# A decoder trunk whose feed-forward blocks use seven products: partial sums kept in PSUM, and products chained from block to block

## The chip, the cores and the metric

The kernel runs on one core of a Trainium2 chip. The metric is the device time of one execution in microseconds (us), lower being better. The core's engines are TensorE (PE, matmuls, with its weight loads shown as PEld), VectorE (DVE), ScalarE (ACT), GpSimd (POOL) and SyncE (SP, which issues most transfers). Matmul results are accumulated in PSUM, which has eight banks; a tile of 128 partitions by 512 float32 values fills one bank.

## What is computed

The reference is a two-layer decoder trunk on 512 tokens of width 1024. Each layer has a feed-forward stage, an attention mix (latent attention in the first layer, sparse attention in the second, both with memory heads), and a second feed-forward stage, each followed by a layer norm. The change touches the four feed-forward stages alone:

```python
def swiglu(x, w_gu, w_down):
    g, u = jnp.split(x @ w_gu, 2, axis=-1)
    return (jax.nn.silu(g) * u) @ w_down

x = layer_norm(DN_ALPHA * x + 0.5 * swiglu(x, w_gu, w_down), ln_g, ln_b)
```

The inner width is 2816, which is 22 chunks of 128 features. All values are float32. The kernel splits each operand into a high part and the remainder (`split`: ACT casts the high part, DVE subtracts to get the low part) and sums three matmuls, high by high, high by low and low by high.

## The kernel before

**Feed-forward.** `ffn` walks over five groups of chunks (`GROUPS`): a letter `s` is a chunk computed directly (`single`), a letter `d` one computed by seven products (`seven`). There are 77 chunks of the second kind in 20 groups of two to five. After a group's chunks come its down products (`by_units`, in the last group `token_major`), which add into the residual through DVE.

A seven-product chunk wants a gate (`gs`) and an up half (`us`) of 128 features for 512 tokens. Each is a sum over two halves of the input features, and the tokens are split in two halves of 256. So there is a 2x2 by 2x2 block product, which a Strassen-Winograd scheme does with seven quarter products in place of eight. Each quarter product (`quarter`, lines 398, 399 and 402) is 12 matmuls of 256 columns into one half of a bank. The token side of the products (`F.t[1]` to `F.t[5]`, and quarters of `xhi`, `xlo`) is formed once per stage. The weight side is formed for each chunk in `combined` (lines 147 to 153) from two loaded tiles, as four units: `g0` (as loaded), `g1` (a sum), `g2` (the difference of that and `g0`) and `g3` (half a unit).

Numbered as in the scheme, the products of a chunk are P1 (`g0`, lower half), P2 (`g0`, upper half), P3 (`g3`), P4 and P5 (`g1`), P6 and P7 (`g2`). Before the change each goes to a half bank of its own: P1 and P2 share a bank, P4 and P5 another, P6 and P7 a third, P3 has a fourth. The sums are made outside PE. ACT copies P1 to `us` (line 581) and DVE makes seven quarter-width adds with one operand in PSUM (lines 582, 591 to 595 and 599). Then ACT does one Silu over 512 columns (line 556), DVE the product with `us` (line 557) and the split into `hhi` and `hlo`.

**Order.** Weights are prepared in the order of `_unit_order`: SP loads a raw tile (`wraw`, four buffers), DVE combines where needed, ACT and DVE split it into `whi` and `wlo`, which have seven buffers in turn (`ring`: three and four). `unit` hands the next one to the products and asks for preparation four units ahead. The program's order is a priority only: a planner lays out each engine's queue from it by when it estimates that operands and buffers are ready, and sets all semaphores. An engine then works its queue in that order. The eight banks are taken round robin (`fbank`), four per chunk.

The lines of the profile speak of helpers: line 201 is every cast of `split`, line 202 every subtraction, lines 434 to 439 are the down products, lines 383 to 388 the directly computed chunks.

Of the kernel before, what the change touches and what calls it, by code (L numbers as in the profile page):

```python
# [9 lines left out]
F32 = mybir.dt.float32  # L10
# [3 lines left out]
ALU = mybir.AluOpType  # L14
# [41 lines left out]
def _unit_order():  # L56
# [2 lines left out]

    def ffn(l, f, s):  # L60
        for m0, items in _groups(l, f):
            m = m0
            for it in items:
                if it == "d":
                    order.extend((f"g{i}", (l, f, m), 1024, s) for i in range(4))
                else:
                    order.extend(("gu", (l, f, m, g), 1024, s) for g in range(2))
                m += 1
            for i in range(m0, m):
                order.append(("dn", (l, f, i), 1024, s))  # L70

# [36 lines left out]
def tile_trunk(ctx: ExitStack, tc, a: dict, out):  # L108
# [12 lines left out]
    class W:  # L121
# [4 lines left out]
        count = 0  # L126
        early = 0
        ready = {}

    def load(src, n=1024):  # L130
        raw = wraw.tile([P, 1024], F32, name="wraw")
# [3 lines left out]
    def combined(name, idx):  # L135


        l, f, m = idx
        lo, up = slice(0, 512), slice(512, 1024)
        op = nc.vector.tensor_tensor  # L140
        if name == "g0":
            W.g = load(a["gu"][l, f, m, 0])
            return W.g
        if name == "g1":
            W.u = load(a["gu"][l, f, m, 1])
            W.s = wraw.tile([P, 1024], F32, name="wraw")
            op(W.s[:, up], W.g[:, lo], W.u[:, lo], op=ALU.subtract)
            op(W.u[:, lo], W.u[:, lo], W.u[:, up], op=ALU.add)
            return W.u
        if name == "g2":  # L150
            op(W.s[:, lo], W.u[:, lo], W.g[:, lo], op=ALU.subtract)
            return W.s
        op(W.g[:, up], W.g[:, up], W.s[:, lo], op=ALU.subtract)
        return W.g[:, up]

    def ring(scope):
        pool, tag = wring, "r"
# [79 lines left out]
    def psum_pool(side, name):  # L237

        old = getattr(PS, side + "_st", None)
        if old is not None:  # L240
            old.close()
        st = ExitStack()
        pool = st.enter_context(tc.tile_pool(name=f"{name}_{side}", bufs=1, space=PSUM, side=side,
                                             reuse_waits="tile"))
        setattr(PS, side, pool)
        setattr(PS, side + "_st", st)

    def bank(i):
        i %= 8
# [82 lines left out]
    def norm_tile(t, st, spill=None, final=False):  # L332
# [15 lines left out]
        def turn():  # L348
            for h in range(2):
                pt = bank((2 * t if t < 2 else 6) + h)  # L350
                for c in range(4):
# [39 lines left out]
    def quarter(ps, w, off, xh, xl, first=None):  # L391


        hi, lo = w
        fh, fl = first or (xh, xl)
        for k in range(4):
            ks = slice(off + k * P, off + (k + 1) * P)
            nc.tensor.matmul(ps, lhsT=hi[:, ks], rhs=(xh if k else fh)[:, k], start=k == 0, stop=False)  # L398
            nc.tensor.matmul(ps, lhsT=hi[:, ks], rhs=(xl if k else fl)[:, k], start=False, stop=False)  # L399
        for k in range(4):  # L400
            ks = slice(off + k * P, off + (k + 1) * P)
            nc.tensor.matmul(ps, lhsT=lo[:, ks], rhs=xh[:, k], start=False, stop=k == 3)  # L402

    def quarters(k, c):
        v = (slice(None), slice(4 * k, 4 * k + 4), slice(256 * c, 256 * c + 256))
# [2 lines left out]
    def token_forms():  # L408
# [52 lines left out]

    def by_units(names, lhs, on_tile, b, look):


        n = len(names)
        tiles = [(b // 2 + i) % NT for i in range(NT)]
# [63 lines left out]
    def ffn(l, f, i, halves, spill=None, final=False, mid=None, hook=None):  # L530
# [14 lines left out]
        for gi, (m0, items) in enumerate(groups):  # L545
# [22 lines left out]
            def seven(j, t4):  # L568

                c0, c1 = slice(0, 256), slice(256, 512)  # L570
                gs = hp.tile([P, T], F32, tag="sg", name="gs", bufs=3)
                us = hp.tile([P, T], F32, tag="sg", name="us", bufs=3)
                op = nc.vector.tensor_tensor
                w0 = unit("g0", (l, f, m0 + j), 4)
                w = unit("g1", (l, f, m0 + j), 4) if t4 == 4 else None
                p12, p45 = fbank(), fbank()
                if t4 == 4:
                    quarter(p45[:, c0], w, 512, *F.t[5 if gi else 4], F.t[4])
                quarter(p12[:, c0], w0, 0, *quarters(0, 0))
                quarter(p12[:, c1], w0, 512, *quarters(1, 0))  # L580
                nc.scalar.copy(us[:, c0], p12[:, c0])
                op(gs[:, c0], us[:, c0], p12[:, c1], op=ALU.add)
                if t4 == 5:
                    w = unit("g1", (l, f, m0 + j), 4)
                    quarter(p45[:, c0], w, 512, *F.t[5])
                quarter(p45[:, c1], w, 0, *F.t[1])
                w = unit("g2", (l, f, m0 + j), 4)
                p67 = fbank()
                quarter(p67[:, c0], w, 0, *F.t[2])
                quarter(p67[:, c1], w, 512, *F.t[3])  # L590
                op(us[:, c0], us[:, c0], p67[:, c0], op=ALU.add)
# [4 lines left out]
                w = unit("g3", (l, f, m0 + j), 4)  # L596
                p3 = fbank()
                quarter(p3[:, c0], w, 0, *quarters(1, 1))
                op(gs[:, c1], gs[:, c1], p3[:, c0], op=ALU.add)
                evac(j, gs, us, gs)  # L600

            j, opened = 0, False
            if gi == 0:
                forms = token_forms() if halves else F.forms
            if gi == 0 and halves:
                ws, ps = [], []
                for j in range(3):
                    for g in range(2):
                        ws.append(unit("gu", (l, f, m0 + j, g), 0))
                        ps.append(fbank())  # L610
                if hook is not None:
                    hook()
# [14 lines left out]
            for it in items:  # L627
                if gi == 0:
                    next(forms, None)
                if it == "d":  # L630
                    if gi == 0:
                        for _ in forms:
                            pass
                        if 5 not in F.t:
                            second_t4()
                    seven(j, 5 if opened else 4)
                    opened = True
                else:
                    single(j)
                j += 1  # L640

            last = gi == len(groups) - 1
            if gi == 2 and mid is not None:
# [971 lines left out]
```

## Time and profile before

| | |
|---|---|
| runs shown | 1841.46, 1841.88 and 1844.01 us, median 1841.88 |
| profiled execution, first to last instruction | 1840.9 us |
| mean granted clock of TensorE | 0.997 |
| busy: PE, PEld, DVE, ACT, POOL | 1822.2, 1641.0, 1462.0, 867.6, 168.5 us |
| matmuls | 12748, of which 6468 belong to the seven-product chunks |
| read from HBM | 188.16 MB, 106 GB/s over the span |

The profiled execution is known by its span alone; the runs' times also hold what lies around the span, which is 1.0 us by the median. A row that groups instructions gives the line, engine, operation, tiles written and read, shapes and count, then the busy time in us, the mean of one in ns, and after the last bar the idle time of that engine just before them with what ended it. A row of the timeline gives start and length in us. "Idle before" is time without an instruction on the engine, and the matmuls' ends are modelled.

### The profile page before, as it was taken

To read this page: it belongs to the slowest core of one execution; us is meant where nothing else is said; L and a number is where in the kernel's file an instruction comes from. 1 tells how busy PE (TensorE), PEld (TensorE's weight loads), DVE (VectorE), ACT (ScalarE), POOL (GpSimd) and SP (SyncE) were. 2 spreads that over 40 slices of the span, in tenths; PEclk is the share of its full clock that TensorE was granted. 3 is DMA by queue.
4 is the path that set the end of the run, shared out by engine and by line. 5 is a ranking of instruction groups with operands and counts; after the bars stand their busy time and mean duration, and the time that the engine had idled before them with its cause. 6 is when DMAs were issued, how large, how long until landed. Compare 5 with 4: busy or idle time off the path is not lost.

```text
span 1840.9 us, 31942 instructions
## 1 busy us (share of the span) xinstructions
PE 1822.2 (99%) x12748; PEld 1641.0 (89%) x12748; DVE 1462.0 (79%) x2364; ACT 867.6 (47%) x1440; POOL 168.5 (9%) x216
## 2 busy tenths in 40 slices
PE   9999999999999999999999999999999999999998
PEld 8899899996789899999998998998956699999997
DVE  8798788758668789788887987987667487887987
ACT  6344345456545335334753433444566354434432
POOL 0000000025500000000100000001266200000000
PEclk9999999999999999999999999999999999999999
DMA  7333335531135233234443323334321324323322
GB/s 267 115 115 110 120 104 152 185 104 33 61 114 173 80 103 127 81 104 149 130 154 104 127 84 112 115 122 160 109 50 25 114 87 145 115 81 115 122 80 74
DMA packets 61669, 208.05 MB, mean 113 GB/s; under 512 B 7152, under 2 KB 8320, under 8 KB 61520
## 3 DMA queue, kind: packets, MB, share of 16 engines
q1 hardware_dynamic: 57568, 194.46, 32.3%
q0 software_dynamic: 3520, 11.16, 1.8%
q8 instruction: 100, 1.64, 0.4%
q14 instruction: 49, 0.40, 0.1%
q10 hardware_dynamic: 432, 0.39, 0.1%
HBM read 188.16 MB, written 7.34 MB: 106 GB/s over the span
## 4 chain that ended last, share of the span: by engine, by line
PE 93%; DVE 2%; ACT 2%; DMA 1%; issue 1%; POOL 1%; POOLq 0%; SPq 0%; DVEq 0%; ACTq 0%
PE bank L398 13%; PE bank L399 13%; PE bank L402 13%; PE bank L435 5%; PE bank L434 5%; PE bank L436 5%; PE bank L437 5%; PE bank L438 5%; PE bank L439 5%; PE bank L383 3%; PE bank L388 3%; PE bank L385 3%; PE tb L715 3%; PE o L743 2%; PE bank L371 2%; PE bank L370 2%
## 5 line engine op out<-in xcount | busy, mean ns | idle before, releaser
L201 ACT CAST whi<-wraw 128x1024 fp32r<-128x1024 f32 (+2 forms) x475 | 460.6, 978 | 534.5 <-PE bank L439 239.5
L202 DVE TENSOR_TENSOR wlo<-wraw,whi 128x1024 fp32r<-128x1024 f32 (+2 forms) x475 | 535.0, 1129 | 125.8 <-ACT whi L201 124.8
L399 PE MATMUL bank<-t,whi 128*128 128x256 f32 x956 | 229.3, 276 | 0.0
L398 PE MATMUL bank<-t,whi 128*128 128x256 f32 x956 | 229.2, 276 | 0.0
L398 PE MATMUL bank<-xhi,whi 128*128 128x256 f32 x924 | 220.9, 276 | 0.0
L399 PE MATMUL bank<-xlo,whi 128*128 128x256 f32 x924 | 220.9, 276 | 0.0
L399 PEld LDWEIGHTS bank<-t,whi 128*128 128x128 f32 x956 | 179.5, 188 | 0.6
L398 PEld LDWEIGHTS bank<-t,whi 128*128 128x128 f32 x956 | 179.5, 188 | 0.6
L399 PEld LDWEIGHTS bank<-xlo,whi 128*128 128x128 f32 x924 | 173.5, 188 | 0.0
L398 PEld LDWEIGHTS bank<-xhi,whi 128*128 128x128 f32 x924 | 173.5, 188 | 0.0
L328 DVE SCALAR_TENSOR_TENSOR x<-x,bank 128x512 f32<-128x512 f32 x176 | 112.1, 681 | 53.3 <-PE bank L438 51.6
L402 PE MATMUL bank<-t,wlo 128*128 128x256 f32 x940 | 144.9, 276 | 0.0
L402 PE MATMUL bank<-xhi,wlo 128*128 128x256 f32 x924 | 142.3, 276 | 0.0
L434 PE MATMUL bank<-whi,hhi 128*128 128x512 f32 x336 | 131.1, 391 | 0.0
L435 PE MATMUL bank<-whi,hhi 128*128 128x512 f32 x336 | 131.0, 390 | 0.0
L436 PE MATMUL bank<-wlo,hhi 128*128 128x512 f32 x336 | 130.9, 389 | 0.0
L438 PE MATMUL bank<-whi,hlo 128*128 128x512 f32 x336 | 130.8, 389 | 0.0
L439 PE MATMUL bank<-whi,hlo 128*128 128x512 f32 x336 | 130.8, 389 | 0.0
L437 PE MATMUL bank<-wlo,hhi 128*128 128x512 f32 x336 | 130.7, 389 | 0.0
L383 PE MATMUL bank<-xhi,whi 128*128 128x256 f32 x520 | 124.8, 281 | 0.2 <-ACT whi L201 0.2
L402 PEld LDWEIGHTS bank<-t,wlo 128*128 128x128 f32 x940 | 124.1, 188 | 0.0
L385 PE MATMUL bank<-xlo,whi 128*128 128x256 f32 x520 | 123.6, 279 | 0.3 <-DVE xlo L202 0.3
(347 smaller groups left out, 3864.4 us busy)
## 6 DMA issues: line engine op xcount, KB each, us to landing
wraw<-in_gu SPq DMA_DIRECT2D x173, 512.0 KB, 3.4
wraw<-in_dn SPq DMA_DIRECT2D x88, 512.0 KB, 3.8
wraw<-in_wo SPq DMA_DIRECT2D x16, 512.0 KB, 4.4
wraw<-in_wm SPq DMA_DIRECT2D x8, 512.0 KB, 4.0
x_dram<-x SPq DMA_DIRECT2D x8, 512.0 KB, 2.6
x<-x_dram SPq DMA_DIRECT2D x8, 512.0 KB, 4.4
wraw<-in_w SPq DMA_DIRECT2D x8, 512.0 KB, 3.8
wraw<-in_wq SPq DMA_DIRECT2D x6, 512.0 KB, 4.3
```

What stands on the lines that cost most here:

```text
L201: nc.scalar.copy(hi, src)
L202: return eng.tensor_tensor(lo, src, hi.bitcast(F32), op=ALU.subtract).ins
L383: nc.tensor.matmul(ps[:, c0:c1], lhsT=hi[:, k * P:(k + 1) * P], rhs=F.xhi[:, k, c0:c1], start=k == 0, stop=False)
L398: nc.tensor.matmul(ps, lhsT=hi[:, ks], rhs=(xh if k else fh)[:, k], start=k == 0, stop=False)
L399: nc.tensor.matmul(ps, lhsT=hi[:, ks], rhs=(xl if k else fl)[:, k], start=False, stop=False)
L402: nc.tensor.matmul(ps, lhsT=lo[:, ks], rhs=xh[:, k], start=False, stop=k == 3)
L434: nc.tensor.matmul(p0, lhsT=ahi, rhs=hi[:, 0:512], start=first, stop=False)
L435: nc.tensor.matmul(p1, lhsT=ahi, rhs=hi[:, 512:1024], start=first, stop=False)
L436: nc.tensor.matmul(p0, lhsT=ahi, rhs=lo[:, 0:512], start=False, stop=False)
L437: nc.tensor.matmul(p1, lhsT=ahi, rhs=lo[:, 512:1024], start=False, stop=False)
L438: nc.tensor.matmul(p0, lhsT=alo, rhs=hi[:, 0:512], start=False, stop=last)
L439: nc.tensor.matmul(p1, lhsT=alo, rhs=hi[:, 512:1024], start=False, stop=last)
```

## The change

The seven sums move into PSUM. A product may now accumulate into the bank of an earlier one (`start=False`), and where a partial sum is needed twice, ACT copies it from its bank to the next one (`seeded`) and PE goes on accumulating on the copy. Each partial sum has a bank of its own, in which the upper half is used (`own`). With P1 in r1, r2 is a copy of r1; r1 takes P2 and is then the first half of the gate. r2 takes P6. In a group's later chunks r3 is a copy of r2 at this point and takes P4, while r2 takes P5, is read by DVE, and takes P3, which gives the gate's second half. P7 is copied to `us` by ACT, and DVE adds r2 and r3 to it. In a group's first chunk P4 has a bank to itself instead, and r2 is copied to `sg` in SBUF and added by DVE. Silu reads the banks directly, in two halves.

A matmul without `start` adds only where an earlier matmul has written the bank since it was last cleared; `PS.set` keeps account of the banks for which that holds, and `seeded` puts in one matmul where it doesn't.

The products of neighbouring chunks are interleaved: the first product (P1) of the following chunk is issued in the middle of the current one, its second (P2) just before the current P3. The order of the products is P4 P1 P7 P2 P6 P1' P5 P2' P3 in a group's first chunk, P6 P7 P1' P5 P4 P2' P3 in a middle one and P6 P7 P5 P4 P3 in the last (a prime marks the following chunk). The order of the weight units follows: `g0 g1 g2 g0' g3`, then `g2 g0' g1 g3`. `combined` keeps the raw tiles of two chunks apart (`W.pairs`), and the token form of P4 changes its sign, so that P4 is added.

```diff
@@ ffn of _unit_order
-                if it == "d":
-                    order.extend((f"g{i}", (l, f, m), 1024, s) for i in range(4))
...
+            for i in range(m, end):
+                names = ("g0", "g1", "g2", "+", "g3") if i == m else ("g2", "+", "g1", "g3")
+                for name in names:
+                    if name != "+":
+                        order.append((name, (l, f, i), 1024, s))
+                    elif i + 1 < end:
+                        order.append(("g0", (l, f, i + 1), 1024, s))
@@ token_forms
-        u = less(u, b[1, 0])
+        u = less(b[1, 0], u)
         form(4, u)
@@ ffn
-                quarter(p12[:, c0], w0, 0, *quarters(0, 0))
-                quarter(p12[:, c1], w0, 512, *quarters(1, 0))
-                nc.scalar.copy(us[:, c0], p12[:, c0])
-                op(gs[:, c0], us[:, c0], p12[:, c1], op=ALU.add)
...
-                op(us[:, c0], us[:, c0], p67[:, c0], op=ALU.add)
-                op(gs[:, c1], us[:, c0], p45[:, c1], op=ALU.add)
-                op(us[:, c0], us[:, c0], p67[:, c1], op=ALU.add)
-                op(us[:, c1], us[:, c0], p45[:, c1], op=ALU.add)
-                op(us[:, c0], us[:, c0], p45[:, c0], op=ALU.subtract)
...
-                op(gs[:, c1], gs[:, c1], p3[:, c0], op=ALU.add)
-                evac(j, gs, us, gs)
+                def own():
+                    PS.set.add(F.bk % 8)
+                    return fbank()[:, c1]
+
+                def seeded(src, w):
+                    bits = F.bk % 8 in PS.set
+                    r = own()
+                    if not bits:
+                        nc.tensor.matmul(r, lhsT=w[0][:, 0:P], rhs=F.xhi[:, 0, c0], start=True, stop=True)
+                    nc.scalar.copy(r, src)
+                    return r
+
+                def m1(j):
+                    if j not in w0:
+                        w0[j] = unit("g0", (l, f, m0 + j), 4)
+                    r1[j] = own()
+                    quarter(r1[j], w0[j], 0, *quarters(0, 0))
+                    r2[j] = seeded(r1[j], w0[j])
+
+                def m2(j):
+                    quarter(r1[j], w0[j], 512, *quarters(1, 0), start=False)
+                    sg[j] = hp.tile([P, T], F32, tag="sg", name="sg", bufs=3)
+                    nc.scalar.activation(sg[j][:, c0], r1[j], AF.Silu)
+
+                def p7(j, w):
+                    e = own()
+                    quarter(e, w, 512, *F.t[3])
+                    nc.scalar.copy(us[j][:, c0], e)
+
+                def p5(j, w):
+                    quarter(r2[j], w, 0, *F.t[1], start=False)
+                    op(us[j][:, c1], us[j][:, c0], r2[j], op=ALU.add)
+
+                def p3(j):
+                    w = unit("g3", (l, f, m0 + j), 4)
+                    quarter(r2[j], w, 0, *quarters(1, 1), start=False)
+                    nc.scalar.activation(sg[j][:, c1], r2[j], AF.Silu)
...
+                    if n == 0:
...
+                        r3 = own()
+                        quarter(r3, w, 512, *F.t[5 if gi else 4], F.t[4])
+                        m1(j)
+                        ws = unit("g2", (l, f, m0 + j), 4)
+                        p7(j, ws)
+                        m2(j)
+                        quarter(r2[j], ws, 0, *F.t[2], start=False)
+                        nc.scalar.copy(sg[j][:, c1], r2[j])
+                        if following is not None:
+                            m1(following)
+                        p5(j, w)
+                        op(us[j][:, c0], us[j][:, c0], r3, op=ALU.add)
+                        op(us[j][:, c0], us[j][:, c0], sg[j][:, c1], op=ALU.add)
+                    else:
+                        ws = unit("g2", (l, f, m0 + j), 4)
+                        quarter(r2[j], ws, 0, *F.t[2], start=False)
+                        r3 = seeded(r2[j], ws)
+                        p7(j, ws)
+                        if following is not None:
+                            m1(following)
+                        w = unit("g1", (l, f, m0 + j), 4)
+                        p5(j, w)
+                        quarter(r3, w, 512, *F.t[5], start=False)
+                        op(us[j][:, c0], us[j][:, c0], r3, op=ALU.add)
+                    if following is not None:
+                        m2(following)
+                    p3(j)
+                    finish(j)
```

More of the change, by code (lines that the diff above doesn't have):

```diff
@@ L61, in ffn @@
         for m0, items in _groups(l, f):
-            m = m0
-            for it in items:
-                if it == "d":
-                    order.extend((f"g{i}", (l, f, m), 1024, s) for i in range(4))
-                else:
-                    order.extend(("gu", (l, f, m, g), 1024, s) for g in range(2))
-                m += 1
+            m = m0 + items.count("s")
+            for i in range(m0, m):
+                order.extend(("gu", (l, f, i, g), 1024, s) for g in range(2))
+            end = m0 + len(items)
+            for i in range(m, end):
[5 more added lines that the diff above has]
+                        order.append(("g0", (l, f, i + 1), 1024, s))
+            m = end
             for i in range(m0, m):
@@ L141, in combined @@
         if name == "g0":
-            W.g = load(a["gu"][l, f, m, 0])
-            return W.g
-        if name == "g1":
[L145 to L149, printed above, removed]
-        if name == "g2":
[L151 to L154, printed above, removed]
+            W.pairs[idx] = [load(a["gu"][l, f, m, 0])]
+            return W.pairs[idx][0]
+        raws = W.pairs[idx]
+        if len(raws) == 1:
+            g, u, d = raws[0], load(a["gu"][l, f, m, 1]), wraw.tile([P, 1024], F32, name="wraw")
+            raws += [u, d]
+            op(d[:, up], g[:, lo], u[:, lo], op=ALU.subtract)
+            op(u[:, lo], u[:, lo], u[:, up], op=ALU.add)
+        g, u, d = raws
+        if name == "g1":
+            return u
+        if name == "g2":
+            op(d[:, lo], u[:, lo], g[:, lo], op=ALU.subtract)
+            return d
+        del W.pairs[idx]
+        op(g[:, up], g[:, up], d[:, lo], op=ALU.subtract)
+        return g[:, up]
     def ring(scope):
@@ L246, in psum_pool @@
         setattr(PS, side + "_st", st)
+        PS.set = set()
     def bank(i):
@@ L350, in turn @@
                 pt = bank((2 * t if t < 2 else 6) + h)
+                PS.set.discard((2 * t if t < 2 else 6) + h)
                 for c in range(4):
@@ L389, in feature_major, with quarter @@
                              start=False, stop=k == NKT - 1)
-    def quarter(ps, w, off, xh, xl, first=None):
+    def quarter(ps, w, off, xh, xl, first=None, start=True):
         hi, lo = w
@@ L462, in by_units @@
     def by_units(names, lhs, on_tile, b, look):
+        PS.set.update(range(8))
         n = len(names)
@@ L566, in single, with sevens @@
                 evac(j, *pp)
[L568 removed]
+            def sevens(js):
                 c0, c1 = slice(0, 256), slice(256, 512)
[L571 to L572 removed]
                 op = nc.vector.tensor_tensor
[L574 to L578, printed above, removed]
[L579 to L600 removed]
@@ L602, in ffn @@
-            j, opened = 0, False
+                us, sg, w0, r1, r2 = {}, {}, {}, {}, {}
+                def own():
+                    PS.set.add(F.bk % 8)
+                    return fbank()[:, c1]
[6 more added lines that the diff above has]
+                    return r
@@ new lines, in finish @@
+                def finish(j):
+                    g = sg[j]
+                    nc.vector.scalar_tensor_tensor(g, g, 0.5, us[j], op0=ALU.mult, op1=ALU.mult)
+                    split(hhi[:, j, :], hlo[:, j, :], g)
+                for n, j in enumerate(js):
+                    us[j] = hp.tile([P, T], F32, tag="sg", name="us", bufs=3)
+                    following = js[n + 1] if n + 1 < len(js) else None
+                    if n == 0:
+                        w0[j] = unit("g0", (l, f, m0 + j), 4)
+                        w = unit("g1", (l, f, m0 + j), 4)
[19 more added lines that the diff above has]
+                            m1(following)
+                        w = unit("g1", (l, f, m0 + j), 4)
+                        p5(j, w)
[5 more added lines that the diff above has]
+                    finish(j)
@@ L603, in ffn @@
+            j = 0
             if gi == 0:
@@ L609, in ffn @@
                         ws.append(unit("gu", (l, f, m0 + j, g), 0))
+                        PS.set.add(F.bk % 8)
                         ps.append(fbank())
@@ L630, in ffn @@
                 if it == "d":
[L631 to L639, printed above, removed]
-                j += 1
+                    break
+                single(j)
+                j += 1
+            if gi == 0:
+                for _ in forms:
+                    pass
+                second_t4()
+            sevens(range(j, n))
             last = gi == len(groups) - 1
```

9 lines of the change are left out of this document (6 added, 3 removed).

## The prediction

> **What bounds the kernel now.** I read the page's totals and chain first, then TensorE's product lines, then stretches of the feed-forward stages.
>
> ```profile
> PE 1822.2 (99%) x12748; PEld 1641.0 (89%) x12748; DVE 1462.0 (79%) x2364; ACT 867.6 (47%) x1440; POOL 168.5 (9%) x216
> PE 93%; DVE 2%; ACT 2%; DMA 1%; issue 1%; POOL 1%; POOLq 0%; SPq 0%; DVEq 0%; ACTq 0%
> ```
>
> TensorE (PE) works 1822.2 of 1840.9 us and makes 93% of the chain. A busy PE may still be badly fed, so next come the groups of the product helper (lines 398, 399, 402); the last column is PE's idle time before them.
>
> ```profile
> L399 PE MATMUL bank<-t,whi 128*128 128x256 f32 x956 | 229.3, 276 | 0.0
> L398 PE MATMUL bank<-t,whi 128*128 128x256 f32 x956 | 229.2, 276 | 0.0
> L398 PE MATMUL bank<-xhi,whi 128*128 128x256 f32 x924 | 220.9, 276 | 0.0
> L399 PE MATMUL bank<-xlo,whi 128*128 128x256 f32 x924 | 220.9, 276 | 0.0
> L402 PE MATMUL bank<-t,wlo 128*128 128x256 f32 x940 | 144.9, 276 | 0.0
> L402 PE MATMUL bank<-xhi,wlo 128*128 128x256 f32 x924 | 142.3, 276 | 0.0
> L398 PE MATMUL bank<-t5h,whi 128*128 128x256 f32 x276 | 66.5, 277 | 0.0
> L399 PE MATMUL bank<-t5l,whi 128*128 128x256 f32 x276 | 66.3, 276 | 0.0
> L402 PE MATMUL bank<-t5h,wlo 128*128 128x256 f32 x292 | 45.0, 276 | 0.0
> ```
>
> The counts add up to 6468, which is 77 seven-product blocks of 84 matmuls. Not one of them is preceded by measurable idle time. So there is no wait in these blocks that could be removed.
>
> ```profile
> 153.00:162.52 9.52, 9.52 (x87) 9.52 (x86) 9.36 (x16) 5.32 (x8) 0.00 (x0) 1.00 0.43 132
> 152.00:170.00 18.00, 18.00 (x161) 18.00 (x161) 17.81 (x30) 9.75 (x13) 0.00 (x0) 1.00 0.35 117
> 361.00:366.00 5.00, 5.00 (x45) 5.00 (x44) 2.25 (x2) 2.18 (x5) 0.00 (x0) 1.00 0.87 351
> 125.50:134.50 9.00, 9.00 (x42) 7.43 (x41) 8.09 (x14) 2.57 (x4) 0.00 (x0) 1.00 0.19 61
> 137.00:146.00 9.00, 9.00 (x41) 7.47 (x40) 3.37 (x5) 2.73 (x3) 0.00 (x0) 1.00 0.18 58
> ```
>
> The columns are length, then busy time (and count) of PE, weight load, VectorE (DVE), ScalarE (ACT) and GpSimd, then PE's granted clock. Inside the blocks PE passes a 256-column matmul about every 0.113 us (18.00 us, 161 counted with about two cut at the edges), so a product of 12 takes 1.36 us and a block of seven 9.52 us. DVE is full there: 9.36 of 9.52 us. It is full and yet holds nobody up.
>
> **The change part by part.** *Matmuls.* Each block still runs seven products of 12: 0 us. A seed put into a bank without its bits costs one extra matmul, 0.113 us. The down products of the inner groups mark all eight banks as set and every product adds its own, so I count one such place, after the shared K/V stage, where the transposes have taken banks out of the set: 0.1 us.
>
> *DVE and ACT work.* Durations are min/median/max in ns, then mean ns in the last two rows.
>
> ```profile
> L581 ACT COPY us<-bank x77: 354/363/371, 45.9 to 1804.7; 128x256 f32<-128x256 f32 x77
> L591 DVE TENSOR_TENSOR us<-us,bank x77: 407/415/422, 50.9 to 1809.6; 128x256 f32<-128x256 f32 x77
> L556 ACT ACTIVATE gs<-gs 128x512 f32<-128x512 f32 x77 | 48.8, 634 | 79.7 <-DVE gs L599 79.7
> L201 ACT CAST whi<-wraw 128x1024 fp32r<-128x1024 f32 x387 | 404.4, 1053 | 370.1 <-PE bank L439 163.7 <-PE bank L399 108.4 <-DVE wraw L148 49.7
> ```
>
> A block has seven quarter adds now; afterwards it has three (first of a group, 20 groups) or two (the other 57). That is 20x4 + 57x5 = 365 adds less, at 0.415 us 151 us of DVE time, all of it under the gapless PE: worth 0 us. DVE falls to about 9.36 - 5x0.415 = 7.3 us per block. ACT gains two copies (0.73 us) and has its one 512-wide Silu cut in two halves (not in the trace; each between the 0.36 of the copy and the 0.63 of the whole; I take the copy's): 5.3 becomes about 6.1 us per block. This too lies under PE; uncovered it would cost 0.8 us x 77 = 62 us, but only PE's own waits can bring that out.
>
> *New waits of PE.* This is the price. Before, nothing that ACT or DVE did with a bank was needed by PE again until the bank came round. Afterwards PE writes a bank again after ACT or DVE has read it, and accumulates on ACT's copy. Counting products that lie between the read's cause and PE's next write:
> - first block of a group: one product in each of four places (second product after the seed copy; fifth after the copy to `sg`; the following block's second after its seed; third after DVE's add);
> - last block: one product in two places (fifth after the seed of r3; third after DVE's add);
> - the 37 middle blocks: two or more everywhere.
>
> So 120 waits have a cover of 1.36 us, of which 80 on ACT and 40 on DVE. What does a reply take? Two fences, DVE then ACT, each with PE's start of the next product (the second PE row of the first):
>
> ```profile
> 114.05 0.62 PE L402 MATMUL bank<-t,wlo 128*128 128x256 f32 x4
> 114.50 0.28 PE L398 MATMUL bank<-xhi,whi 128*128 128x256 f32 x1
> 114.70 0.42 DVE L591 TENSOR_TENSOR us<-us,bank 128x256 f32<-128x256 f32 x1 [0.25 <-PE bank L402]
> ...
> 124.02 0.28 PE L398 MATMUL bank<-xhi,whi 128*128 128x256 f32 x1
> 125.38 0.41 DVE L591 TENSOR_TENSOR us<-us,bank 128x256 f32<-128x256 f32 x1
> ...
> 174.38 0.28 PE L398 MATMUL bank<-xhi,whi 128*128 128x256 f32 x1
> 175.13 0.41 DVE L591 TENSOR_TENSOR us<-us,bank 128x256 f32<-128x256 f32 x1
> ```
>
> ```profile
> 151.26 0.28 PE L398 MATMUL bank<-t,whi 128*128 128x256 f32 x1
> 151.58 0.36 ACT L581 COPY us<-bank 128x256 f32<-128x256 f32 x1
> ...
> 118.58 0.28 PE L398 MATMUL bank<-t5h,whi 128*128 128x256 f32 x1
> 119.33 0.36 ACT L581 COPY us<-bank 128x256 f32<-128x256 f32 x1
> ...
> 17.50 1.05 ACT L201 CAST whi<-wraw 128x1024 fp32r<-128x1024 f32 x1 [2.64 <-DMA wraw<-in_gu]
> 18.61 0.38 PE L383 MATMUL bank<-xhi,whi 128*128 128x256 f32 x1 [0.22 <-ACT whi L201]
> ```
>
> A free DVE starts 0.20 us into the next product (114.70 - 114.50), a free ACT 0.32 us in. PE follows a release by about 0.05 us (18.61 after 17.50 + 1.05). So DVE may be late by 1.36 - 0.20 - 0.42 - 0.05 = 0.69 us and ACT by 1.36 - 0.32 - 0.36 - 0.05 = 0.63 us before PE stops. Seen lateness: DVE 0, 1.16 and 0.55 us in the three places, which is 0, 0.47 and 0 us of stall, mean 0.16; ACT 0.43 us in the second place, behind a weight cast: no stall. Behind a whole cast just begun ACT would be 1.05 us late: 0.42 us of stall.
>
> Where they fall: the first block follows the down products, where DVE is busy 3.37 of 9.00 us and ACT 2.73, so I take 0 for its 80 waits. For the last block I take the mean of the three rows, 20 x 0.16 = 3.1 us, and halve it because DVE then has two idle us per block where it had 0.16: 1.6 us. For its seed I let one in ten meet a fresh cast: 20 x 0.42 / 10 = 0.8 us. The middle blocks allow 1.36 us more, which none of these rows reaches: 0. Bounds: below 0; above, all 20 last blocks paying both (20 x 0.89 = 17.8 us) and all 20 first ones the DVE stall (9.4 us): 27 us. I take 1.6 + 0.8 because the ordinary rows lie within the allowance.
>
> What is queued behind a late copy: on ACT the weight casts, needed by PE a block later; on DVE the low halves of those weights. Neither is urgent, unless rival B holds.
>
> The Trainium skill ("ScalarE: Activation LUTs", the step-by-step section) says that ACT writes to PSUM with less latency than to SBUF. No row here has ACT writing PSUM; by it the seed copies are shorter than 0.36 us, ACT's allowance grows and its 0.8 us shrinks towards 0.
>
> *Elsewhere.* The planner may order the attention stages a little differently. PE's listed waits, nearly all of them there, sum to about 10 us, the longest being
>
> ```profile
> PE tb L715 <- POOL pp L1317: 2.2, 1, 2.2
> ```
>
> I take 0 and allow 2 us either way.
>
> **Sum.** 0.1 + 0 + 1.6 + 0.8 = 2.5 us on a span of 1840.9. The median of the runs, 1841.88, lies 1.0 us above the span, which is launch and end around it and stays. So 1841.9 + 2.5 = 1844.4 us, +0.14%. A measurement of this kernel can tell about 0.2%, 3.7 us, so I forecast no change that can be measured.
>
> **Rivals.**
>
> *A, slower: the one-product covers don't hold.* It decides from 0.69 us of lateness on DVE and 0.63 on ACT, in the last block of each group. For it: 1.16 us is already seen on DVE, and ACT works more than before. Against: DVE has become freer. If half of the 20 last blocks pay 0.89 us and some first ones too, it is 9 us: 1851; if all do, 18 us: 1860. Chance 0.30.
>
> *B, slower: weights late.* The new order holds three raw buffers of a block and the next block's first one at once, which is all four.
>
> ```profile
> wraw<-in_gu SPq DMA_DIRECT2D x173, 512.0 KB, 3.4
> L151 DVE TENSOR_TENSOR wraw<-wraw 128x512 f32<-128x512 f32 x77 | 52.7, 684 | 0.5
> L202 DVE TENSOR_TENSOR wlo<-wraw,whi 128x1024 fp32r<-128x1024 f32 (+2 forms) x475 | 535.0, 1129 | 125.8 <-ACT whi L201 124.8
> ACT whi L201 <- PE bank L399: 185.9, 177, 2.6
> ```
>
> If the next load must wait for the last of them, a block's preparation is load 3.4, three combinations 2.05, cast 1.05 and three low halves 3.4 us, with 2.2 us of other DVE work between: 12.1 against PE's 9.52, 2.6 us lost per following block. The seven ring buffers let a unit's cast start eight products (10.9 us) ahead of its use, which after cast and low half (2.2) leaves 8.7 us. That absorbs the 3 x 2.6 of a group of four and not the 4 x 2.6 of the four groups of five: 4 x 1.7 = 7 us, and some more where a seed queues on ACT behind a cast that waits for DVE. Against: the difference's buffer comes back before the two low halves, and today casts wait for PE, not for data (the last row). 1850, chance 0.09.
>
> *C: it doesn't do what it says.* If seeds needed a matmul in every place (77 + 57 seeds), 134 x 0.113 = 15 us: 1857. Against: the set of banks above. Chance 0.03.
>
> *D, faster.* If DVE's reads of PSUM slowed the matmuls, fewer of them would speed PE up. The stretches above speak against it: 42 matmuls in 9.00 us with DVE at 8.09 and 41 with DVE at 3.37; 161 in 18.00 and 45 in 5.00 us at a full and a half-empty DVE. What is left is 2 us or more of PE's waits elsewhere and noise: 1837, chance 0.08.
>
> The Trainium skill ("TensorE: Matmul & The Clock Gate", Back-to-back issue gap) gives 256 columns 256/2.4 + 2.5 = 109.2 ns where the trace has 113; by that rule 6468 x 4 ns = 26 us would be open, and the time 1816, if the change touched what takes them. The stretches say that it does not.
>
> **How the numbers follow.** No change 0.50, at 1844.4 (own range 1839 to 1846); A 0.30, B 0.09, C 0.03, D 0.08. Faster is D, 0.08; slower A, B and C, 0.42. The range reaches down to the 2 us of the other stages, 1839.5, and up through A's half case to most of its full one, 1857; about 0.05 is left out below and 0.1 above.
>
> **What would show it.** Right: the idle time before the product lines stays under 3 us in all, DVE loses about 150 us of busy time, and the blocks keep 9.52 us. A: PE waits that name ACT's copy or DVE's add in the last blocks. B: PE waiting for weights, or ACT's casts waiting for the weight differences in most blocks. C: more than a few matmuls beyond 12748. Wrong altogether: matmuls in the blocks at a pitch other than 0.113 us.

## The result and the profile after

The changed kernel takes 1864.85 us (median of four runs, 1863.76 to 1867.71) where the kernel before takes 1841.74 (four runs too, 1841.46 to 1844.01): 1.0124 times as long, 95% interval 1.0110 to 1.0138. It is slower by some 23 us, and outside the range. The profiled executions are 1862.5 and 1840.9 us, 21.6 apart.

First the page's totals after, then the groups of the product helper (now lines 409, 411 and 415) with the weight load that precedes one of them; the columns are those of before.

```profile
PE 1837.0 (99%) x12749; PEld 1653.1 (89%) x12749; DVE 1346.2 (72%) x1999; ACT 910.0 (49%) x1671; POOL 170.0 (9%) x216
...
L409 PE MATMUL bank<-t,whi 128*128 128x256 f32 x956 | 232.6, 279 | 0.3 <-ACT bank L598 0.3
L411 PE MATMUL bank<-t,whi 128*128 128x256 f32 x956 | 232.5, 279 | 0.0
L409 PE MATMUL bank<-xhi,whi 128*128 128x256 f32 x924 | 226.2, 281 | 6.0 <-DVE us L620 4.7
L411 PE MATMUL bank<-xlo,whi 128*128 128x256 f32 x924 | 223.7, 278 | 0.0
L409 PEld LDWEIGHTS bank<-xhi,whi 128*128 128x128 f32 x924 | 174.0, 188 | 10.6 <-DVE us L620 8.4
L415 PE MATMUL bank<-t,wlo 128*128 128x256 f32 x940 | 146.7, 279 | 0.0
L415 PE MATMUL bank<-xhi,wlo 128*128 128x256 f32 x924 | 143.8, 278 | 0.0
```

Two things differ. Idle time stands before line 409, the first matmul of a product, and most of it waits for line 620, DVE's `us c1 = us c0 + r2` in `p5`. And every group's mean has grown from 276 to 278-281 ns, also the groups that never wait. The totals say the same in another way: PE is busy 14.8 us longer with one matmul more.

The waits of PE, after (total, times, longest), the rows of the feed-forward stages:

```profile
PE bank L409 <- DVE us L620: 4.7, 6, 1.6
...
PE bank L397 <- DVE xlo L212: 2.3, 1, 2.3
PE bank L409 <- ACT bank L598: 1.4, 3, 0.6
```

Line 598 is the seed copy in `seeded`. Here is a wait in the last block of a group, in the timeline after:

```profile
196.08 0.68 DVE L212 TENSOR_TENSOR hlo<-sg,hhi 128x512 fp32r<-128x512 f32 x1
196.14 0.28 PE L409 MATMUL bank<-t5h,whi 128*128 128x256 f32 x1
...
196.68 1.22 DVE L212 TENSOR_TENSOR wlo<-wraw,whi 128x1024 fp32r<-128x1024 f32 x1
...
197.09 0.63 PE L415 MATMUL bank<-t5h,wlo 128*128 128x256 f32 x4
...
197.81 0.41 DVE L620 TENSOR_TENSOR us<-us,bank 128x256 f32<-128x256 f32 x1
...
198.28 0.39 PE L409 MATMUL bank<-xhi,whi 128*128 128x256 f32 x1 [0.56 <-DVE us L620]
```

P5 is done when P4 starts at 196.14. The add that reads it stands in DVE's queue behind two subtractions and begins at 197.81, 1.47 us later than a free DVE would (196.14 + 0.20). P3 begins at 198.28. In 17 of the 20 groups the planner has even put one down matmul ahead of P3, and PE waits behind that.

The second kind is hard to see. The timeline around P3 of a first block, after; the rows at 297.00 and 297.11 are the product ahead of it, P2':

```profile
297.00 0.19 PEld L409 LDWEIGHTS bank<-xhi,whi 128*128 128x128 f32 x1
297.11 0.28 PE L409 MATMUL bank<-xhi,whi 128*128 128x256 f32 x1
...
297.30 0.69 DVE L163 TENSOR_TENSOR wraw<-wraw 128x512 f32<-128x512 f32 x1
...
297.91 0.41 DVE L620 TENSOR_TENSOR us<-us,bank 128x256 f32<-128x256 f32 x1
298.01 0.62 PE L415 MATMUL bank<-xhi,wlo 128*128 128x256 f32 x4
...
298.38 0.19 PEld L409 LDWEIGHTS bank<-xhi,whi 128*128 128x128 f32 x1
298.47 0.30 PE L409 MATMUL bank<-xhi,whi 128*128 128x256 f32 x1
298.60 0.28 PE L411 MATMUL bank<-xlo,whi 128*128 128x256 f32 x1
298.72 0.28 PE L409 MATMUL bank<-xhi,whi 128*128 128x256 f32 x1
```

No wait is listed for that P3. Its first weight load begins behind DVE's add, 0.09 us ahead of its matmul where that of P2' begins 0.11 ahead. By the trace's unrounded starts P3's first matmul still comes 114 ns after the one before it, and the second 132 ns after the first, some 20 ns late. From there the matmuls follow each other every 0.118 us. Stretches of 18 us, after (columns as in the prediction):

```profile
152.00:170.00 18.00, 18.00 (x162) 18.00 (x161) 14.81 (x22) 8.96 (x17) 0.00 (x0) 1.00 0.30 99
300.00:318.00 18.00, 18.00 (x155) 18.00 (x154) 14.73 (x22) 10.70 (x20) 0.00 (x0) 1.00 0.62 201
```

With about two cut at the edges, 160 and 153 matmuls: 113 and 118 ns, with PE always busy, the granted clock at 1.00 in both and DVE equally busy. This slow pitch goes on to the end of the group's products, 227 or 311 matmuls later.

So I sorted the 6468 product matmuls of each trace by the distance from their start to that of the next matmul. The first four rows of numbers are counts.

| distance | before | after |
|---|---|---|
| up to 115.5 ns (mean 113.3) | 6350 | 3809 |
| 115.5 to 122 ns (mean 117.8 after) | 106 | 2587 |
| 122 to 200 ns | 12 | 51 |
| 200 ns or more | 0 | 21 |
| sum of distances | 733.8 us | 750.3 us |

Of the 16.5 us, 2481 x 4.5 ns = 11.2 are slow pitch, 6.9 - 21 x 0.113 = 4.5 are long gaps, and 39 short ones by some 25 ns are 1.0. Another 5.6 us lie between the moved down matmuls and P3 (the distances from a down matmul to a product grew by 9.8, those among down matmuls fell by 4.3). That makes 22.1; the other stages give back 0.5. **Stalls are 10 us and slow pitch is 11**; the short waits themselves are the 1.0. Eight of the first blocks' P3 begin a slow stretch, 1984 of the 2587 matmuls; P2 of a first block at 974 us begins another of 203.

### The profile page after: what moved, and what is told of

Read it like the earlier page. It is cut to its first block, busy times and chain, and to the rows that moved or that the text cites. A ratio compares the mean times of both kernels' runs of the same rounds, so it can differ in the third digit from the quotient of the medians.

```text
span 1862.5 us, 31652 instructions
## 1 busy us (share of the span) xinstructions
PE 1837.0 (99%) x12749; PEld 1653.1 (89%) x12749; DVE 1346.2 (72%) x1999; ACT 910.0 (49%) x1671; POOL 170.0 (9%) x216
## 5 line engine op out<-in xcount | busy, mean ns | idle before, releaser
L409 PE MATMUL bank<-t,whi 128*128 128x256 f32 x956 | 232.6, 279 | 0.3 <-ACT bank L598 0.3
L411 PE MATMUL bank<-t,whi 128*128 128x256 f32 x956 | 232.5, 279 | 0.0
L409 PE MATMUL bank<-xhi,whi 128*128 128x256 f32 x924 | 226.2, 281 | 6.0 <-DVE us L620 4.7
L395 PE MATMUL bank<-xhi,whi 128*128 128x256 f32 x520 | 124.7, 281 | 0.0
```

The costliest lines, as they stand in the source:

```text
L395: nc.tensor.matmul(ps[:, c0:c1], lhsT=hi[:, k * P:(k + 1) * P], rhs=F.xhi[:, k, c0:c1], start=k == 0, stop=False)
```

## The experiments

The texts on record name their theories by letters, which hold for one text only and are not the prediction's letters. Their counts of 3600 or 3622 slow matmuls after and 951 before take in all stages. The table has all kernels, each compared with runs of the kernel before that were timed beside it (medians 1841.27 to 1842.00 for the experiments); "slow" counts product matmuls at 115.5 to 122 ns, "long" those with 200 ns or more, and the last column is the sum of the distances. These three are of the one profiled execution, which for both and best lay 3.6 and 2.6 us above the median. Of the long ones of both and actread 14 and 15 are matmuls of 213 ns at half the clock (last section), not waits, and odd64's 20 are the distance behind P3's first matmul, 200 ns each.

| kernel | median us | to before, 95% | slow | long | products us |
|---|---|---|---|---|---|
| before | 1841.74 | | 106 | 0 | 733.8 |
| after | 1864.85 | 1.0110-1.0138 | 2587 | 21 | 750.3 |
| lastown | 1851.13 | 1.0039-1.0069 | 1493 | 8 | 743.0 |
| p4late | 1865.38 | 1.0117-1.0147 | 1460 | 30 | 748.6 |
| both | 1857.47 | 1.0076-1.0106 | 2141 | 27 | 750.0 |
| orderonly | 1849.79 | 1.0026-1.0059 | 103 | 1 | 734.7 |
| nofirst | 1866.70 | 1.0117-1.0151 | 5763 | 0 | 758.8 |
| odd64 | 1867.44 | 1.0126-1.0160 | 5112 | 20 | 757.8 |
| nooffset | 1847.95 | 1.0018-1.0042 | 1011 | 0 | 739.4 |
| unlock | 1864.02 | 1.0106-1.0136 | 2379 | 26 | 750.7 |
| actread | 1852.04 | 1.0041-1.0071 | 659 | 28 | 743.6 |
| best | 1856.51 | 1.0069-1.0099 | 2216 | 10 | 748.3 |
| best2 | 1850.64 | 1.0032-1.0062 | 558 | 14 | 741.4 |

**The last block alone (lastown).** The last chunk of a group goes back to sums outside PSUM, in this order of products and with two products to a bank, so that its P3 no longer waits for the add that reads r2.

```diff
+                    elif following is None:
+                        quarter(r2[j], ws, 0, *F.t[2], start=False)
+                        nc.scalar.copy(sg[j][:, c1], r2[j])
+                        e, q = fbank(), fbank()
+                        quarter(e[:, c0], ws, 512, *F.t[3])
...
+                        quarter(q[:, c0], w, 0, *F.t[1])
+                        quarter(q[:, c1], w, 512, *F.t[5])
+                        op(us[j][:, c1], us[j][:, c0], q[:, c0], op=ALU.add)
...
+                        quarter(e[:, c1], w, 0, *quarters(1, 1))
```

> The changed kernel with the last chunk of each group summed outside PSUM as it was before (P5, P4, P7 and P3 in banks of their own, two banks as now, DVE adds), so that no product of the last chunk waits for DVE's add or for a seed copy. Theory W: PE's stalls ahead of the last P3 (6 us, and about 2 us in the matmul after each of them) and the waits on the seed in front of the last P5 (0.5 us) go, the slow pitch that begins in the first chunks stays: 1855 to 1859. Rival O: 1862 to 1868. Rival S: the 20 seeds and 40 accumulated products less of 134 seeds buy a sixth to a quarter of the loss: 1858 to 1861, and the pitch of the last chunks alone falls.

Measured 1851.13 us: 13.7 us of the 23 came back, more than expected. The stalls at the last P3 are gone from the list, where one long wait for a seed is left:

```profile
PE bank L409 <- ACT bank L598: 1.6, 1, 1.6
```

The products are still 9.2 us longer than before (743.0 - 733.8), of which slow pitch is 1387 x 4.5 ns = 6.2: the short waits at the first P3 remain. That more came back than expected is in part luck: slow pitch is 4.9 us less than after the change though the edit leaves the first blocks alone, since six first P3s turned the pitch here and mostly not the same ones.

**The first block's P4 moved (p4late), and both edits (both).** In the first block P4 goes behind P5, so that the first block's P3 gets a second product as cover.

```diff
-                names = ("g0", "g1", "g2", "+", "g3") if i == m else ("g2", "+", "g1", "g3")
+                names = ("g0", "g2", "+", "g1", "g3") if i == m else ("g2", "+", "g1", "g3")
...
-                        quarter(r3, w, 512, *F.t[5 if gi else 4], F.t[4])
                         m1(j)
...
                         p5(j, w)
+                        r3 = own()
+                        quarter(r3, w, 512, *F.t[5 if gi else 4], F.t[4])
```

> The changed kernel with one thing moved: in a group's first chunk product P4 comes after P5 and not at the front (weight units g0 g2 g0' g1 g3), so that P3 follows DVE's add by two products and not one. Theory W (short waits): the changed kernel loses time where a product waits some tens of ns for ACT or DVE, mostly because the matmuls after such a wait run at a pitch of 117.8 and not 113.4 ns until the stream is broken again; nearly all of these stretches begin at the first chunk's P3. With that wait gone the matmuls at 117.8 ns fall from about 3600 to under 1600 and the time falls by 8 to 11 us to 1854 to 1857. Rival O (order): the new order of weight units and raw tiles costs the time; it stays: 1862 to 1868. Rival S (seeds): matmuls that add onto a bank that ACT has written, or ACT's writes into PSUM, slow PE; nothing of that changes here: 1862 to 1868, pitch as it was.

> Both edits together: P4 after P5 in the first chunk, and the last chunk of a group summed outside PSUM. Theory W: nearly no wait of PE for ACT or DVE is left in the chunks, fewer than 1500 matmuls at 117.8 ns, 1841 to 1846. Rival O: 1860 to 1868. Rival S: 1855 to 1862.

Both missed, by 8 us and more than 11. In p4late slow pitch fell by 5.1 us (1127 matmuls), but the stalls grew: PE's list has 6.4 us for line 620 and 3.6 for seeds, where the changed kernel's has 4.7 and 1.4. The short waits at the first P3 did go: no distance of 127 to 150 ns is left there. But now 16 groups, all but each stage's first, begin at the slow pitch and keep it for exactly 72 matmuls, six products, until P4 comes. Two stretches of 9 us from p4late, one before and one behind the start of P4 (PE's count, then its clock):

```profile
149.80:158.80 9.00, 9.00 (x78) 1.00 0.27 92
158.90:167.90 9.00, 9.00 (x82) 1.00 0.29 97
```

Nothing waits at 158.9. So P4 itself changes the pitch, and a theory that knew only waits had to be dropped. What is special in this P4 stands in the helper: its first two matmuls read `F.t[4]` and the other ten `F.t[5]`, a copy of it in another pool (`quarter(..., *F.t[5], F.t[4])`). The kernel before has this too, as the first product of every group behind the first.

**The order without the sums (orderonly).** The new order of products and weights, with every product in a half bank of its own and the old seven adds.

```diff
-                    r1[j] = own()
-                    quarter(r1[j], w0[j], 0, *quarters(0, 0))
-                    r2[j] = seeded(r1[j], w0[j])
+                    p12[j] = fbank()
+                    quarter(p12[j][:, c0], w0[j], 0, *quarters(0, 0))
```

> The order of the changed kernel alone: products chained over chunks and weight units in the new order, but every product in a half bank of its own and all seven sums made by ACT and DVE as before the change; no seeds, no accumulation across products. Theory W: PE has nothing to wait for, pitch 113.4 ns throughout the chunks, 1840 to 1844. Rival O: the loss is here too, 1855 or more, with PE waiting for weights or ACT's casts waiting for the differences. Rival S: 1840 to 1844.

Measured 1849.79 us, between the theories. The products keep their 734.7 us and 103 slow matmuls, so the order of products and weights costs the products nothing, and no weight is late. The 8 us lie behind the products: the down matmuls take 7.1 us more. PE's list has 4.8 us of waits for a block's sums and casts there, most of it for the gate's last add (line 644) before Silu and the split:

```profile
PE bank L448 <- DVE gs L644: 3.0, 2, 1.9
```

Another 1.6 us are eight down matmuls at half the clock (granted clock 0.51 from 866.7 to 870.2 us), soon after the longest of these waits. The changed kernel's list has no such row, which fits a DVE with 365 adds fewer (72% busy, 78% in orderonly).

**The pitch without the change (nofirst).** The kernel before, with one argument removed: P4 of the first block reads one copy throughout.

```diff
-                    quarter(p45[:, c0], w, 512, *F.t[5 if gi else 4], F.t[4])
+                    quarter(p45[:, c0], w, 512, *F.t[5 if gi else 4])
```

> The kernel before, with the first block's P4 reading one copy of xlo throughout. Theory U (products that follow the down products start slow, and the mixed start of P4 is what puts them to 113 ns): many stretches of the block at 117.8 ns without any accumulation over products, 10 to 25 us more than the kernel before: 1851 to 1867 us. Theory B (the slow pitch comes from accumulating over several products in a bank): 1841 to 1843, with the slow matmuls at the 951 of before.

Measured 1866.70 us, 25 us slower, as much as the change itself, with no accumulation, no new wait and the same work. The same group of five blocks, before and then in nofirst, with the same columns as above:

```profile
147.80:194.70 46.90, 46.90 (x416) 46.90 (x416) 45.77 (x74) 25.25 (x34) 0.00 (x0) 1.00 0.48 159
```

```profile
148.00:197.40 49.40, 49.40 (x421) 49.37 (x420) 46.85 (x76) 26.28 (x35) 0.00 (x0) 1.00 0.46 152
```

PE is busy all the time in both, at 113 and 118 ns. Slow pitch alone is (5763 - 106) x 4.5 ns = 25.5 us here, which is the whole loss. So the pitch of a stream of equal matmuls can have two values, which value it has is settled where the stream starts, and it stays until something turns it. Behind the down products it starts slow (but for each stage's first group), and the mixed P4 is what turns it.

**A step of another length (odd64).** The kernel before, with one 64-column matmul ahead of P3 in each group's first block, overwritten by P3.

```diff
+                if t4 == 4:
+                    nc.tensor.matmul(p3[:, 0:64], lhsT=w[0][:, 0:P], rhs=F.xhi[:, 0, 0:64], start=True, stop=True)
```

> The kernel before, with one matmul of 64 columns (overwritten by the product) ahead of P3 of each group's first block: 20 of them, about 2 us if they cost a pitch each; no sum, no copy and no wait is changed. Theory P (the products' pitch is a phase which any step of another length than a product's matmul can shift, a short wait among them): the blocks after it run at 117.8 ns, some 250 to 340 matmuls of each group by 4.4 ns, 22 to 28 us: 1862 to 1872. Theory Q (only a wait does it): 1842 to 1845.

Measured 1867.44 us. Twenty short matmuls cost 25 us, 22.5 of them (5006 matmuls) because the products behind them run at the slow pitch to the group's end (stretches before and behind the added matmul of the group above, PE's count and clock):

```profile
149.50:157.10 7.60, 7.60 (x69) 1.00 0.41 137
157.40:165.00 7.60, 7.60 (x66) 1.00 0.39 125
```

It stands before the same product at which the changed kernel has its short waits, and does what they do, without a wait. That is what I had missed: a disturbance of a few tens of ns there costs about 1 us.

**Where the copy lies (nooffset).** The kernel before without the spare tile ahead of `F.t[5]`, so that it lies 192 bytes lower.

```diff
-        tp.tile([P, 48], F32, name="offset")
```

> The kernel before, without the spare tile of 48 numbers a partition that stands ahead of F.t[5] in its pool, so that this copy of xlo lies 192 bytes lower. Theory A (what the mixed start of the first P4 does depends on where the two copies lie against each other): the products stay at 117.8 ns from each group's start, as with no mixed start: 1860 to 1868 us. Theory C (that the copy changes between two matmuls is enough): 1841 to 1843.

Measured 1847.95 us, neither: the mixed P4 still turns the pitch, and the slow matmuls come in runs of 12 to 14, one P4 each, at 119 to 120 ns. These 905 more slow matmuls by 5.8 ns are 5.3 of the products' 5.6 us. So the place of an operand changes the pitch of its own product, and turning the stream does not hang on this distance.

**Turning at every P4 (unlock).** The changed kernel, with the mixed start in the P4 of every middle and last block too.

```diff
-                        quarter(r3, w, 512, *F.t[5], start=False)
+                        quarter(r3, w, 512, *F.t[5], F.t[4], start=False)
```

> The changed kernel, with the P4 of every later block also starting on the other copy of xlo (F.t[4] for its first matmul), as that of the first block does. Theory U (this start of P4 puts the products back to 113 ns): slow stretches last no longer than to the next P4, the slow matmuls fall from 3622 towards the 951 of before, the waits stay as they are: 1852 to 1857 us. Theory N (what ends a slow stretch is a break of the stream, and the operand's copy does nothing): 3622 within 300 and 1863 to 1867 us.

Measured 1864.02 us: no gain, but not for the reason that theory N gives. Three stretches between the P4s of one group, in unlock:

```profile
149.00:166.00 17.00, 17.00 (x152) 17.00 (x151) 13.73 (x21) 9.89 (x18) 0.00 (x0) 1.00 0.29 93
167.00:176.00 9.00, 9.00 (x79) 9.00 (x78) 7.66 (x11) 5.56 (x10) 0.00 (x0) 1.00 0.35 118
177.00:185.50 8.50, 8.50 (x78) 8.50 (x77) 7.52 (x11) 5.76 (x10) 0.00 (x0) 1.00 0.52 160
```

By the starts these run at 113.3, 117.8 and 113.4 ns: the mixed start turns a slow stream fast and a fast one slow. It is a switch to the other value, not a reset, so it can't repair what it doesn't know of.

**Who reads r2 (actread).** The changed kernel with an ACT copy as reader of r2; DVE's add then works from SBUF.

```diff
-                    op(us[j][:, c1], us[j][:, c0], r2[j], op=ALU.add)
+                    nc.scalar.copy(us[j][:, c1], r2[j])
+                    op(us[j][:, c1], us[j][:, c1], us[j][:, c0], op=ALU.add)
```

> The changed kernel, but the read of r2 that the next product waits for is an ACT copy to SBUF, and VectorE adds from SBUF afterwards. Theory L (the late reader is VectorE's add; each wait of 20 to 50 ns at the first block's P3 leaves the products at 117.8 ns until the stream breaks): the waits for that add (4.7 us before the products of L409) fall below 1 us, the stall of about 2 us at the last block's P3 mostly goes, and the count of slow matmuls falls from 3622 to under 2000: 1847 to 1853 us. Theory B (the slow pitch belongs to accumulation over several products in a bank, whoever reads): the stalls go but the slow pitch stays: 1854 to 1858. Theory A (ACT, with one copy more a block, is late itself): waits move to ACT and the time stays at 1862 to 1867.

Measured 1852.04 us, 12.8 us of the 23 back, with the same accumulation in the banks. PE's list has no wait for line 620 any more, and the slow matmuls fall from 2587 to 659. So the short waits at P3 were what made most products slow, and accumulation was not. What is left is 2.5 us of slow pitch, 1.5 us of matmuls at half the clock, and waits for the seed:

```profile
PE bank L409 <- ACT bank L598: 3.9, 5, 2.0
```

**Together (best, best2).** best2 is lastown with the ACT reader in the other blocks; best has the mixed start in every P4 as well.

> Last block summed outside PSUM (two products to a bank there), r2 read by an ACT copy in the other blocks, and every P4 starting on the other copy. If L and U both hold, nothing waits at a P3 and slow stretches end at the next P4: 1841 to 1846 us, like the kernel before. If only the last block's stalls matter (lastown had 1851.1): 1849 to 1852. If ACT is late itself: 1853 or more.

> The changed kernel with its last block summed outside PSUM (two products to a bank there) and r2 read by an ACT copy in the other blocks; every P4 after the first block's starts on one copy, as in the changed kernel. Theory W+L (two causes: stalls at the last block's P3, and short waits at the first block's P3 that leave the products at 117.8 ns): both are gone, slow matmuls in the products fall from 2587 to under 300, and the time is 1841 to 1846 us. Theory B (accumulation over several products costs pitch by itself): 1849 to 1853.

best took 1856.51 us, best2 1850.64. In best no first P3 comes late, so the mixed starts have nothing to mend and turn good streams slow (2216). best2 has 558 slow matmuls and one listed wait of 0.5 us, for ACT's copy of P7, whose bank the last P3 shares there. It missed its 1841 to 1846 and lies in the range of theory B, but not by that theory's cause, since slow pitch is the smaller part of what is left. Its products are 7.6 us longer than before: 2.0 of slow pitch and 7.1 - 14 x 0.113 = 5.5 of long gaps, most of them behind a late seed (3.0 us in four listed waits), as in this timeline of best2:

```profile
964.32 1.99 ACT L211 CAST whi<-wraw 128x1024 fp32r<-128x1024 f32 x2 [7.25 <-DVE wraw L160]
966.22 0.61 ACT L211 CAST hhi<-sg 128x512 fp32r<-128x512 f32 x1
966.74 0.36 ACT L598 COPY bank<-bank 128x256 f32<-128x256 f32 x1
...
967.16 0.39 PE L409 MATMUL bank<-xhi,whi 128*128 128x256 f32 x1 [1.55 <-ACT bank L598]
```

The seed waits behind two weight casts and a cast of `hhi` that ACT got late. The rest of the 9.1 us between the spans, 1.5 us, lies outside the products. No version I ran is faster than the kernel before.

## Why the prediction was wrong, point by point

- **Bound by PE, DVE's relief worth nothing.** Right. DVE lost its 365 adds (2364 to 1999 instructions), and the time rose. Its busy time fell by 115.8 us where I had 151: the mean lengths of adds that run back to back overlap, so that count times mean says too much (at 197.81 above, the add begins 0.09 us before the subtraction ahead of it ends). In the new order the relief is worth something: with the adds kept (orderonly) the down products took 7.1 us more. ACT rose by 42.4 us, 0.55 a block for my 0.8.
- **Matmuls.** Right: 12749.
- **The allowance on DVE, 0.69 us.** Too large by 0.1: the wait stands at the product's first weight load, not at its matmul. At 298 us the load began at 298.38 and the matmul at 298.47. The add was 0.60 us late there (297.91 for 297.11 + 0.20), inside my allowance, and PE was held.
- **First blocks at 0.** Wrong. I argued from DVE's ease behind the down products, but P3 is the group's ninth product, and there DVE is at its weight work again (line 163 above): the add was 0.60 us late in 15 of the 20. At as many first P3s the distance from the first matmul to the second was 131 to 136 ns, and eight of these turned the pitch. Two waits of 0.7 us by the starts, for the seed, also stood in first blocks, before P2.
- **Last blocks at 1.6 us of DVE stall and 0.8 of seed.** Mis-sized: all stalls together came to 10 us, some 2 of them before products that wait for a seed and the rest in the last blocks' P3. My halving ("DVE then has two idle us") failed, since the idle time does not lie where the add is queued. In 19 of the 20 last blocks the add was 0.74 to 2.66 us late, over the allowance, and 1.2 in the mean of all, where my three rows had 0.57. By the prediction's own rule (lateness less 0.69) that is 11 us, of which the 17 moved down matmuls, 0.23 us each, cover up to 4. One middle block's P3, which I had at 0, was some 50 ns late (at 180 us) and turned the pitch. Rival A had this with 9 us for its half case, and its place was right.
- **The step that failed most** is one that I never wrote as a term: that a wait costs its own length. In this stream a wait of 20 ns costs 4.5 ns for each of the next 227 or 311 matmuls, 1.0 to 1.4 us. A's half case gave 1851; of the 14 us from there to the measured 1864.85, 11 are slow pitch. I had named a pitch other than 0.113 us as what would make the prediction wrong altogether, and it did.
- **Rival D and the stretches.** They were right that DVE's load doesn't set the pitch, and so is the pair of stretches after (14.81 and 14.73 us of DVE). But I went on to hold the pitch for fixed, from stretches of blocks that all lay in one group, which the mixed P4 had turned fast. The Trainium skill ("TensorE: Matmul & The Clock Gate", Back-to-back issue gap) gives one value for 256 columns, 109.2 ns by its formula for the isolated gap. The runs have two, 113.3 and 117.8 ns.
- **Rival B.** Not seen: lines 411 and 415 have 0.0 idle, what line 409 waits for is DVE's add and ACT's copy, and the new order alone (orderonly) left the products at 734.7 us.
- **Rival C.** No: one matmul more.
- **The seed copy's price.** The two copies of ACT after, to PSUM and to SBUF:

```profile
L598 ACT COPY bank<-bank 128x256 f32<-128x256 f32 x134 | 48.7, 363 | 63.5 <-PE bank L415 63.2
...
L616 ACT COPY us<-bank 128x256 f32<-128x256 f32 x77 | 28.1, 365 | 18.0 <-PE bank L415 18.0
```

363 ns in the mean, against 365. By the Trainium skill ("ScalarE: Activation LUTs", the step-by-step section) the first should be the shorter; the trace agrees by 2 ns, which changes nothing.

## What to carry to other kernels

When PE never pauses, look at its pitch as well as at its waits: a difference of 4 ns a matmul does not show in a busy share and here was half of the loss. Before PE is made to wait for another engine inside a gapless stream, work out how late that engine's queue can be at that very place, measured to the weight load, and don't price a short wait at its own length. An argument that looks idle, like the mixed start of one product, can hold a kernel's speed, so take it away once to see what it is worth.

## What the runs showed of the hardware

- A stream of equal matmuls of 256 columns ran at 113.3 or at 117.8 ns, at a granted clock of 1.00, and kept its value for hundreds of matmuls. It was changed by waits of some 20 ns, by one matmul of 64 columns, and by a change of the moving operand's place within a product. What it is in the machine these runs don't tell. Nor do they say why one short wait turns it and another does not: of 15 such waits at first P3s after the change eight did, and distances of 132 and 135 ns were in both sets. But one thing goes with it. In the first blocks of after, lastown and unlock, a distance of 131 to 136 ns behind P3's first matmul turned the stream in all 17 cases in which that matmul had come 113 or 114 ns after the one before it, and in none of the 26 in which it had come 115 to 119 ns after. (In lastown two distances of 127 and 128 ns, behind 119, turned it too.)
- A stall of 2 us can cost a second time by the clock. In actread PE stood idle for 2.0 us (the longest of its waits above) and then had a granted clock of 0.58 (actread's stretches: PE's count, then its clock):

```profile
190.80:193.10 2.30, 0.34 (x4) 1.00 0.26 69
193.10:196.60 3.50, 3.50 (x18) 0.58 0.85 265
```

Eighteen matmuls took 3.50 us, in which 31 pass at 0.113 us each. The same was seen in both behind a wait of 2.2 us (both's stretches):

```profile
966.40:968.90 2.50, 0.32 (x3) 1.00 0.44 167
968.90:972.50 3.60, 3.58 (x17) 0.53 0.43 146
```

A wait of 2.2 us in p4late left the clock at 1.00, so length alone doesn't decide it (p4late's stretches):

```profile
970.00:972.50 2.50, 0.30 (x4) 1.00 0.42 159
972.50:976.00 3.50, 3.50 (x30) 1.00 0.49 150
```

The Trainium skill ("TensorE: Matmul & The Clock Gate", the part on the clock gate) tells of a fall to half speed after an idle window of about 3.4 us; here 2.0 us of idle time were enough in one run and 2.2 in another.
